# Low parts of weights from VectorE to GpSimd in the second half, and the last quarter's norm factors moved past the first gates

## The chip, the cores and the metric

The kernel runs on one core of a Trainium2 chip. The time is that of one execution on the device in microseconds (us), the median over the runs of a kernel. The engines are TensorE (PE, its weight loads PEld), VectorE (DVE), ScalarE (ACT), GpSimd (POOL) and SyncE (SP), which issues all DMAs. Each engine works through its own queue in order.

## What is computed

One step of a small decoder trunk: a pooling layer (stage A), one projection that gives keys and values to all, and one attention layer (stage B), for 2048 prompt positions and 8 sample positions, model width 1024, 16 heads of 64 in each of three groups of dilation 1, 4 and 16.

```
u, gate = rmsnorm(h, g_a) @ w_a_in                      # 1024 -> 2 x 1024
h = h + (pool_residual(u) @ w_group * scale * silu(gate)) @ w_a_out
kv = rmsnorm(h, g_kv) @ w_kv                            # 1024 -> 3 groups x 2 x 1024, rope on k
q, gate = rmsnorm(h, g_b) @ w_b_in                      # 1024 -> 3 x 1024 + 1024, rope on q
o, lse = windowed attention of each group (128 keys of the block, 128 before)
h = h + (sum over groups of softmax(lse) * o * silu(gate)) @ w_b_out
y = rmsnorm(h, g_final)
```

All is float32. A product runs on TensorE in a shorter float (the type `F32R`) with split operands: each operand is a high part, its rounded copy, and a low part, what the rounding left; a product is high times high, high times low and low times high.

## The kernel before

Activations lie with the width on the partitions, positions along the row. Stage A goes through four quarters of 512 positions (the first with the 8 sample columns). Of each quarter it computes 8 units of `u`, 8 of the gate and, in `run_o`, 8 of the output projection, a unit being one block of 128 output columns: 24 matmuls of 128x512 (eight blocks of the width, three terms). The output of `run_o` is h after the layer; ScalarE squares it, GpSimd adds the squares up in `acc2`, and after the eighth unit `rstd_from` makes of them the factors 1/rms of all positions: four one-column matmuls with a column of ones (L261), a handful of small VectorE instructions around a square root on ScalarE (L262 to L269), a 128x512 diagonal (L270), a matmul that spreads it over the partitions (L280) and a copy (L281). For the last quarter this call was deferred by two ticks, and `close_a` flushes what is deferred, so that it stood between stage A and stage B.

Stage B first takes half 0 (1024 positions): 8 gate units beside which `make_t` builds sums of blocks of the activations (the tiles `t0`, `t1`), then pairs of heads in a form with seven products in place of eight that reads these tiles, then half 1: for each of 8 pairs of heads `p` and three groups units of k, q and v, and 8 gate units at the end. From the last unit of p = 0 on, the attention of the prompt runs beside the units of half 1: at each tick (eight matmuls of a unit, six ticks a unit) one step of `prompt_attn`. A step covers two blocks of 128 queries of one head: score matmuls (L1211, they read the tile `qt`, whose lower half GpSimd copies to the upper partitions in L1163), masking and minimum on VectorE (L1218), exponential on ScalarE (L1224), transposes (L1232), high part on ScalarE (L1244) and low part on VectorE (L1248) of the transposed weights, product with v (L1273 to L1278) and the sum of its two halves on VectorE (L1301).

The weights of a unit come by DMA into a staging tile `wst` of 128x1024, GpSimd scales them by the norm's gain (L127), ScalarE rounds them into `ringh` (L163), and an engine chosen per unit subtracts to get `ringl` (L168). In half 1 there is a single staging tile, so the load of the weights after next waits for L168 of the next. The ring holds the weights of two units. The order within a unit is that of `plan`: at its start the next unit's weights are scaled, one tick later rounded, two ticks later subtracted, and the load of those after next is issued.

```
def lo(self):
    for k in ((0, KT),) if self.eng is pool else ((0, KH2), (KH2, KT)):
        k = slice(*k)
        self.eng.tensor_sub(self.w[1][:, k], self.st[:, k], self.w[0][:, k].bitcast(F32))
...
    at(0, nxt.scale)
    at(int(nxt.gs is not None), nxt.hi)
    at(2 if nxt.gs is not None else 1, nxt.lo)
```

So VectorE does a low part in two instructions of 128x512, GpSimd in one of 128x1024. In stage A the low parts are GpSimd's, in stage B VectorE's. The buffer pool `nwork` has one buffer with the tag `xk`; in stage A `norm_b` uses it, later `make_t` for its temporary `tmp`. The program order written here is not the order on the engines: when the program is built, a list scheduler lays the instructions of each engine out by its own estimate of when they can start, keeping the dependences. A change in one place thus moves instructions in others.

Of the kernel before, what the change touches and what calls it, by code (L numbers as in the profile page):

```python
# [12 lines left out]
F32 = mybir.dt.float32  # L13
# [5 lines left out]
P = 128  # L19
D = 1024  # L20
KT = D // P
SEQ = 2048
NB = 8
HALF = 1024
TOT = SEQ + NB
NQ = 4
QN = SEQ // NQ
# [26 lines left out]
def step_kernel(ctx: ExitStack, tc: tile.TileContext, a: dict):  # L54
    nc = tc.nc
    vec, act, pool, pe = nc.vector, nc.scalar, nc.gpsimd, nc.tensor
# [32 lines left out]
    rpool = low_ctx.enter_context(tc.tile_pool(name="rpool", bufs=1))  # L89
# [3 lines left out]
    rstd2 = {}  # L93
    hn2 = {}
    N = type("N", (), {})()
# [124 lines left out]
    def q_chunks(q):  # L220
        return Q0_CHUNKS if q == 0 else Q_CHUNKS
# [27 lines left out]
    def rstd_from(acc, rstd, n, diag):  # L249
        for _ in rstd_steps(acc, rstd, n, diag):  # L250
            pass
# [36 lines left out]
    def do(fn, *args):  # L288
        items.append(lambda: fn(*args))

    def unit(src, gs, eng, run):
        items.append(Unit(src, gs, eng, run))

    def defer(ticks, fn):
        deferred.append([ticks, fn])
# [18 lines left out]
    def side(gen, rate, name=None):  # L314
        sides.append([gen, rate, 0.0, name])
# [79 lines left out]
    def q_pieces(q):  # L395

        col = q * QN + (NB if q >= 2 else 0)
        return [(col, 0, QN)] + ([(HALF, QN, NB)] if q == 0 else [])

    def q_len(q):  # L400
        return QN + (NB if q == 0 else 0)
# [18 lines left out]
    def work_tile(name, tag="w", bufs=None):  # L420
        return N.work.tile([P, 16 + QN + NB], F32, tag=tag, name=name, bufs=bufs)

    def load_x(q, k):
        xk = work_tile("xk")
        for c0, o, m in q_pieces(q):
            load_dma(xk[:, o:o + m], a["xT"][k, :, c0:c0 + m])
        return xk
# [157 lines left out]
    def run_o(q, ct):  # L585
        def run(w):
            n = q_len(q)
            if ct == 0:
                N.acc2 = work_tile("acc2", "acc", 1)
            xk = load_x(q, ct)  # L590
            acc2 = N.acc2

            def ev(ps, c0, c1):
                vec.tensor_add(xk[:, c0:c1], ps[:, :c1 - c0], xk[:, c0:c1])
                if c1 < n:
                    return
                for d0, o, m in q_pieces(q):
                    store_dma(h1d[ct][:, d0:d0 + m], xk[:, o:o + m])
                if ct == 0:
                    act.activation(acc2[:, :n], xk[:, :n], AF.Square)  # L600
                else:
                    sq = work_tile("sq2")
                    act.activation(sq[:, :n], xk[:, :n], AF.Square)
                    pool.tensor_add(acc2[:, :n], acc2[:, :n], sq[:, :n])
                if ct == KT - 1:
                    r2 = rstd2[q] = rpool.tile([P, QN + NB], F32, tag="rstd2", name="rstd2", bufs=2)
                    defer(2, lambda: rstd_from(acc2, r2, n, work_tile("nv")))
            yield from dense(w, N.y, q_chunks(q), ev, tags=A_TAGS, order=by_term(KT, 0 if ct else 2))
        return run
# [107 lines left out]
    def close_a():  # L717
# [2 lines left out]
        finish()  # L720
        N.actx.close()

    do(close_a)


    def perm(ap, g):
# [102 lines left out]
    def run_qk(hf, kind, g, p):  # L829
        def run(w):  # L830
            raw = raw_tile()
            if kind == 1:
                N.rope = Rope(hf, g)
            rp = N.rope

            def ev(ps, qq, o, m, smpl):
                act.activation(in_order(raw, g, o, m), as_order(ps, g, m), AF.Copy)  # L837
                if smpl:
                    vec.tensor_copy(smp[:, p, kind, g], ps[:, m:m + NB])
                if o + m == HALF:  # L840
                    defer(1, lambda: rp.gather(kind, p, raw))
            yield from dense_h(hf, w, ev)
        return run
# [39 lines left out]
    def run_v(hf, g, p):  # L883
        def run(w):
            vT = [N.bw.tile([P, QN], F32, tag="v", name="vT", bufs=2) for _ in range(2)]

            def ev(ps, qq, o, m, smpl):
                act.activation(vT[qq][:, o - qq * QN:o - qq * QN + m], ps[:, :m], AF.Copy)
                if smpl:
                    vec.tensor_copy(smp[:, p, 2, g], ps[:, m:m + NB])  # L890
                if o + m == (qq + 1) * QN:
                    defer(2, lambda: turn_v(hf, g, p, qq, vT[qq]))
            yield from dense_h(hf, w, ev)
        return run
# [91 lines left out]
    def source(kind, g, p):  # L986
        if kind == 0:
            return a["wQ"][g * NPAIR + p], gq
        return a["wKV"][(2 * g + kind - 1) * NPAIR + p], gvec[:, G_KV]
# [127 lines left out]
    for p in range(NPAIR):  # L1117
        for g in range(3):
            for kind in (1, 0):
                unit(*source(kind, g, p), vec, run_qk(1, kind, g, p))  # L1120
            unit(*source(2, g, p), vec, run_v(1, g, p))
            if p == 0 and g == 2:
                N.attn_unit = sum(not callable(it) for it in items)
                do(start_attention)
# [495 lines left out]
```

## Time and profile before

| | |
|---|---|
| time, median of 3 runs | 3468.94 us (3465.72 to 3475.48) |
| the profiled execution | 3453.65 us, its span 3451.6 us |
| mean granted TensorE clock | 0.969 |
| PE busy | 3187.5 us, 92% of the span |
| DVE, ACT, POOL busy | 2000.7, 1715.3, 1680.1 us (58%, 50%, 49%) |
| mean DMA rate | 173 GB/s |
| half 1 with the attention, 1790 to 3200 us | PE 1338.8 of 1410 us busy, DVE 791.8, ACT 981.2, POOL 712.1 |

A busy share is the share of the time in which an engine has an instruction at work. TensorE's matmuls overlap each other, so that a row's duration is longer than the distance to the next one: eight matmuls of 128x512 in a row take 2.0 us at the full clock.

### The profile page before, as it was taken

What the parts mean: (1) busy time and instruction counts of PE and PEld (TensorE: products, weight loads), DVE (VectorE), ACT (ScalarE), POOL (GpSimd) and SP (SyncE); (2) the same over time, 40 slices, a digit from 0 to 9 for tenths busy, and PEclk for the clock granted to TensorE, in tenths of its full rate; (3) what the DMA queues carried; (4) which work ended last, traced back from release to release, by engine and by line L of the source; (5) the groups of instructions that cost most, each with busy time, mean ns of one, the idle gap of its engine ahead of it and who ended that gap; (6) DMA issues with size and microseconds to landing.
All of it is one profiled execution on the core that took longest, in us unless ns stands there. A gap on an engine that the chain in (4) does not pass through costs nothing.

```text
span 3451.6 us, 56978 instructions
## 1 busy us (share of the span) xinstructions
PE 3187.5 (92%) x19608; PEld 2799.4 (81%) x19608; DVE 2000.7 (58%) x3989; ACT 1715.3 (50%) x3812; POOL 1680.1 (49%) x1026
## 2 busy tenths in 40 slices
PE   8999899899998998987989999999999999999798
PEld 8887678699887887877778877888787888887698
DVE  6745665526767667676426555656464646564345
ACT  3333433324434443334227766776666676778221
POOL 5566765624234354343454454545454645552342
PEclk9999999999999999999999999999999999999899
DMA  4434443434576766767777767687777777774653
GB/s 135 145 129 159 141 156 110 129 98 135 154 185 209 177 193 180 201 198 201 195 206 205 194 187 187 189 201 196 181 194 181 198 182 194 196 199 131 192 155 120
DMA packets 547744, 596.96 MB, mean 173 GB/s; under 512 B 216904, under 2 KB 407752, under 8 KB 547448
## 3 DMA queue, kind: packets, MB, share of 16 engines
q1 hardware_dynamic: 547456, 593.32, 61.7%
q8 instruction: 156, 2.56, 0.3%
q14 instruction: 132, 1.08, 0.1%
HBM read 371.77 MB, written 184.04 MB: 161 GB/s over the span
## 4 chain that ended last, share of the span: by engine, by line
PE 32%; DMA 11%; DVE 5%; ACT 4%; SPq 3%; issue 3%; POOL 2%; DVEq 0%; POOLq 0%; ACTq 0%
PE psd L241 20%; PE pss L1211 3%; PE ppt L1232 3%; PE ppo L1276 1%; PE ppo L1278 1%; DMA spb<-pd 1%; DMA statd<-st 1%; ACT pr L1224 1%; DMA vr<-vd 1%; DMA raw<-xs 1%; DMA qt<-qd 1%; DMA wst<-in_wKV 1%; PE ppo L1273 1%; DVE xs L791 1%; DMA cyt<-yd 1%
## 5 line engine op out<-in xcount | busy, mean ns | idle before, releaser
L1163 POOL CAST qt<-qt 64x1024 fp32r<-64x1024 f32 x192 | 207.1, 1079 | 435.1 <-DMA qt<-qd 371.9
L1224 ACT ACTIVATE pr<-pr,st 128x256 f32<-128x256 f32 (+1 forms) x768 | 345.9, 453 | 126.0 <-DVE st L1218 124.7
L1218 DVE CUSTOM_DVE_ANT_0 pr<-pss,mask 128x256 f32<-128x256 f32 (+1 forms) x768 | 248.5, 360 | 175.7 <-PE pss L1211 118.5
L1248 DVE TENSOR_TENSOR pl<-ppt,ph 128x512 fp32r<-128x512 f32 (+2 forms) x384 | 216.1, 570 | 190.0 <-ACT ph L1244 187.2
L168 POOL TENSOR_TENSOR ringl<-wst,ringh 128x1024 fp32r<-128x1024 f32 x96 | 241.6, 2519 | 124.0 <-ACT ringh L163 72.5
L1211 PE MATMUL pss<-kt,qt 128*128 128x256 f32 (+1 forms) x1536 | 261.2, 288 | 12.8 <-DVE st L1218 7.8
L127 POOL TENSOR_TENSOR wst<-wst,gvec 128x1024 f32<-128x1024 f32 x88 | 177.3, 2017 | 184.8 <-DMA wst<-in_wKV 99.1
L241 PE MATMUL psd<-hn_2h,ringh 128*128 128x512 f32 x640 | 259.2, 405 | 6.6 <-ACT raw L837 5.0
L241 PE MATMUL psd<-hn_3h,ringh 128*128 128x512 f32 x640 | 260.9, 408 | 4.1 <-ACT hn_3h L643 2.4
L163 ACT ACTIVATE ringh<-wst 128x1024 fp32r<-128x1024 f32 x184 | 193.3, 1052 | 139.2 <-PE psd L241 94.9
L241 PE MATMUL psd<-hn_2l,ringh 128*128 128x512 f32 x640 | 257.2, 402 | 5.1 <-DVE hn_2l L644 5.1
L241 PE MATMUL psd<-hn_3l,ringh 128*128 128x512 f32 x640 | 259.4, 405 | 2.5 <-DVE hn_3l L644 2.5
L241 PE MATMUL psd<-hn_2h,ringl 128*128 128x512 f32 x640 | 258.7, 404 | 0.0
L241 PE MATMUL psd<-hn_3h,ringl 128*128 128x512 f32 x640 | 258.4, 404 | 0.0
L1211 PEld LDWEIGHTS pss<-kt,qt 128*128 128x128 f32 x1536 | 223.2, 194 | 29.4 <-DVE st L1218 8.7
L1232 PE MATMUL ppt<-ident,pr 128*128 128x128 f32 x1200 | 209.6, 281 | 36.0 <-DVE pl L1248 23.0
L1244 ACT ACTIVATE ph<-ppt 128x512 fp32r<-128x512 f32 (+2 forms) x384 | 189.7, 500 | 91.6 <-PE ppt L1232 87.1
L168 DVE TENSOR_TENSOR ringl<-wst,ringh 128x512 fp32r<-128x512 f32 x176 | 148.4, 878 | 139.5 <-ACT ringh L163 139.3
L970 PE MATMUL pwx<-t1h,ringh 128*128 128x256 f32 (+1 forms) x576 | 171.1, 297 | 26.4 <-DVE pairl L924 14.0
L1232 PEld LDWEIGHTS ppt<-ident,pr 128*128 128x128 f32 x1200 | 143.1, 142 | 63.1 <-issue 22.5
L1190 POOL TENSOR_TENSOR vt<-vr,vt 128x512 fp32r<-128x512 f32 (+1 forms) x96 | 136.4, 1421 | 80.8 <-ACT vt L1189 72.4
L1276 PE MATMUL ppo<-ph,vt 128*128 128x128 f32 (+1 forms) x688 | 167.6, 274 | 7.6 <-ACT ph L1244 5.7
(301 smaller groups left out, 9828.3 us busy)
## 6 DMA issues: line engine op xcount, KB each, us to landing
qt<-qd SPq DMA_DIRECT2D x192, 256.0 KB
wst<-in_wKV SPq DMA_DIRECT2D x72, 512.0 KB
kt<-kd SPq DMA_DIRECT2D x288, 128.0 KB
wst<-in_wA SPq DMA_DIRECT2D x64, 512.0 KB
wst<-in_wQ SPq DMA_DIRECT2D x52, 512.0 KB
kd<-rh SPq DMA_DIRECT2D x48, 512.0 KB
qd<-rh SPq DMA_DIRECT2D x48, 512.0 KB
vd<-vt SPq DMA_DIRECT2D x96, 256.0 KB
```

Source lines behind the costliest of these rows:

```text
L127: pool.tensor_tensor(st, st, gs[:, :, None].to_broadcast([P, KT, P]), OP.mult)
L163: act.activation(self.w[0], self.st, AF.Copy)
L168: self.eng.tensor_sub(self.w[1][:, k], self.st[:, k], self.w[0][:, k].bitcast(F32))
L241: pe.matmul(ps[:, :n], u[:, k, ws], v[:, k, c0:c1], start=(k, i) == order[0], stop=(k, i) == order[-1])
L1163: pool.tensor_copy(qr[64:128], qr[0:64])
L1211: pe.matmul(ps[:, sl], qt[:, x, qc], kt_[:, kc], start=x == 0, stop=x == 1)
L1218: vec.tensor_tensor_reduce(pr[:, lo:], ps[:, sl], mask[:, lo:], 1.0, BIG, OP.add, OP.min, st[:, 0, h, col:col + 1])
L1224: act.activation(pr[:, lo:], pr[:, lo:], AF.Exp, bias=st[:, 0, h, col:col + 1], scale=-1.0, accum_out=st[:, 1, h, col:col + 1])
L1232: pe.transpose(pt[:, (2 * bb + x) * P:(2 * bb + x + 1) * P], pr[:, x * P:(x + 1) * P], ident)
L1244: act.activation(PB[i][0][:, s], pv[:, s], AF.Copy)
L1248: vec.tensor_sub(PB[i][1][:, s], pv[:, s], PB[i][0][:, s].bitcast(F32))
L1276: pe.matmul(po[:, q0:q1], vt[:, kb + 1, h].rearrange("p x d -> p (x d)"), xh, start=first, stop=False, skip_group_check=True)
```

## The change

In half 1, all units of the pairs of heads with p > 0 (63 units: 7 pairs, three groups, k, q and v) get their low part from GpSimd. The units of p = 0 and the 8 gate units keep VectorE. For the last quarter, the sum of squares and the diagonal get their place in the `xk` buffer of `nwork`, and the norm factors are made by a side generator that starts after `close_a`, lets two ticks pass, issues the sums and the small instructions, waits for three more ticks and issues the spreading matmul and its copy, beside the first gate units.

```diff
             n = q_len(q)
-            if ct == 0:
+            if ct == 0 and q < NQ - 1:
                 N.acc2 = work_tile("acc2", "acc", 1)
+            elif ct == 0:
+                both = N.nwork.tile([P, 2, QN + NB], F32, tag="xk", name="acc3")
+                N.acc2, N.nv3 = both[:, 0], both[:, 1]
             xk = load_x(q, ct)
...
-                if ct == KT - 1:
+                if ct == KT - 1 and q == NQ - 1:
+                    rstd2[q] = rpool.tile([P, QN + NB], F32, tag="rstd2", name="rstd2", bufs=2)
+                elif ct == KT - 1:
                     r2 = rstd2[q] = rpool.tile([P, QN + NB], F32, tag="rstd2", name="rstd2", bufs=2)
                     defer(2, lambda: rstd_from(acc2, r2, n, work_tile("nv")))
...
+    def last_rstd():
+
+        yield
+        yield
+        yield from rstd_steps(N.acc2, rstd2[NQ - 1], QN, N.nv3, 3)
+
     do(close_a)
+    do(lambda: side(last_rstd(), 1.0, "r3"))
...
             for kind in (1, 0):
-                unit(*source(kind, g, p), vec, run_qk(1, kind, g, p))
-            unit(*source(2, g, p), vec, run_v(1, g, p))
+                unit(*source(kind, g, p), pool if p else vec, run_qk(1, kind, g, p))
+            unit(*source(2, g, p), pool if p else vec, run_v(1, g, p))
```

What this does to the engines' queues stands below at three places. Line numbers from L588 on shift by up to 12 in the changed kernel.

TensorE where stage A ends, before: the first gate unit's matmuls (`hn_0`, `hn_1` are the normed activations of the first two quarters), the norm factors, the gate's second half.

```order
L241 MATMUL psd<-hn_0h,ringl 128x264 x8
L261 MATMUL psn<-ones,acc_5203 128x1 x4
L280 MATMUL psn<-nv,ones 128x512
L241 MATMUL psd<-hn_1h_3585,ringh 128x512 x4
L241 MATMUL psd<-hn_1h_3586,ringh 128x512 x4
```

The same place after.

```order
L241 MATMUL psd<-hn_0h,ringl 128x264 x6
L261 MATMUL psn<-ones,acc_5203 128x1 x4
L241 MATMUL psd<-hn_0h,ringl 128x264 x2
L241 MATMUL psd<-hn_1h_3585,ringh 128x512 x4
L241 MATMUL psd<-hn_1h_3586,ringh 128x512 x4
L241 MATMUL psd<-hn_1l_3587,ringh 128x512 x4
L241 MATMUL psd<-hn_1l_3588,ringh 128x512 x4
L241 MATMUL psd<-hn_1h_3585,ringl 128x512 x4
L241 MATMUL psd<-hn_1h_3586,ringl 128x512 x4
L241 MATMUL psd<-hn_0h,ringh 128x256 x8
L241 MATMUL psd<-hn_0l,ringh 128x256 x4
L280 MATMUL psn<-acc_5203,ones 128x512
```

Between the sums (L261) and the spreading matmul (L280) there now stand 24 matmuls of 128x512 and 14 smaller ones; before there was nothing.

VectorE at the same place, before: `make_t` (L668 to L687, its `tmp` in the `xk` buffer) and the norm factors' small instructions. One of the two halves of the `tmp` chain was laid out earlier, in the last quarter of stage A.

```order
L668 TENSOR_TENSOR tmp<-hn_1h_3585,hn_0h 128x2x512
L676 TENSOR_TENSOR tmp<-hn_0h,hn_0l 128x2x8
L669 TENSOR_TENSOR tmp<-tmp,hn_1l_3587 128x2x512
L263 TENSOR_SCALAR rs_5509<-psn 128x4
L670 TENSOR_TENSOR tmp<-tmp,hn_0l 128x2x512
L265 RECIPROCAL rs_5511<-rs_5510 128x4
L266 TENSOR_TENSOR rs_5510<-rs_5511 128x4
L267 TENSOR_TENSOR rs_5510<-rs_5510,rs_5509 128x4
L268 TENSOR_SCALAR rs_5510<-rs_5510 128x4
L269 TENSOR_TENSOR rs_5511<-rs_5511,rs_5510 128x4
L270 TENSOR_TENSOR nv<-ident,rs_5511 128x512
L674 TENSOR_TENSOR tmp<-hn_1h_3586,tmp 128x2x512
```

VectorE after (L673 is what was L668, L690 what was L685).

```order
L270 TENSOR_TENSOR acc_5203<-ident,rs_5590 128x512
L690 TENSOR_TENSOR tmp_5738<-hn_1h_3586,hn_1h_3585 128x1024
L168 TENSOR_TENSOR ringl<-wst,ringh 128x512 x2
L691 TENSOR_TENSOR tmp_5738<-tmp_5738,hn_1l_3588 128x1024
L673 TENSOR_TENSOR tmp<-hn_1h_3585,hn_0h 128x2x512
L681 TENSOR_TENSOR tmp<-hn_0h,hn_0l 128x2x8
L281 COPY rstd_5502<-psn 128x512
L692 TENSOR_TENSOR tmp_5738<-tmp_5738,hn_1l_3587 128x1024
L674 TENSOR_TENSOR tmp<-tmp,hn_1l_3587 128x2x512
L675 TENSOR_TENSOR tmp<-tmp,hn_0l 128x2x512
L168 TENSOR_TENSOR ringl<-wst,ringh 128x512 x2
L679 TENSOR_TENSOR tmp<-hn_1h_3586,tmp 128x2x512
```

The `tmp` chain now begins only behind the norm factors, since these hold the one `xk` buffer until L280 has read it, and both of its halves come after.

GpSimd at the start of the attention, in the second pair of heads, before: scaling (L127), the copies of `qt` (L1163), the low parts of v (L1190) and of rotated k and q (L815).

```order
L127 TENSOR_TENSOR wst<-wst,gvec 128x1024
L1163 COPY qt<-qt 64x1024
L1190 TENSOR_TENSOR vt<-vr,vt 128x10x64
L1163 COPY qt<-qt 64x1024 x2
L127 TENSOR_TENSOR wst<-wst,gvec 128x1024
L1190 TENSOR_TENSOR vt<-vr,vt 128x10x64
L790 TENSOR_TENSOR xs<-xs,cs_5539 128x1024
L1163 COPY qt<-qt 64x1024
L1190 TENSOR_TENSOR vt<-vr,vt 128x8x64
L1163 COPY qt<-qt 64x1024
```

GpSimd after (L1175 is what was L1163, L1202 what was L1190, L827 what was L815).

```order
L127 TENSOR_TENSOR wst<-wst,gq 128x1024
L1202 TENSOR_TENSOR vt<-vr,vt 128x10x64
L1175 COPY qt<-qt 64x1024
L827 TENSOR_TENSOR raw<-raw,rh 128x1024
L1175 COPY qt<-qt 64x1024
L168 TENSOR_TENSOR ringl<-wst,ringh 128x1024
L1175 COPY qt<-qt 64x1024
L1202 TENSOR_TENSOR vt<-vr,vt 128x10x64
L1175 COPY qt<-qt 64x1024 x2
L127 TENSOR_TENSOR wst<-wst,gvec 128x1024
L1202 TENSOR_TENSOR vt<-vr,vt 128x10x64
L1175 COPY qt<-qt 64x1024
```

Per unit there is now one low part (L168) more in GpSimd's queue, with copies of `qt` behind it, and two fewer in VectorE's.

## Rows read from the trace of the kernel before

**Rows 1.** Two stretches: length, busy us (instructions) PE PEld DVE ACT POOL, clock, DMA

```profile
669.00:688.00 19.00, 8.22 (x26) 5.37 (x26) 14.31 (x17) 4.34 (x7) 10.10 (x5) 0.64 0.14 47
1790.00:3200.00 1410.00, 1338.80 (x8400) 1156.40 (x8399) 791.75 (x2383) 981.17 (x2536) 712.12 (x479) 0.98 0.72 188
```

**Rows 2.** Timeline of PE, end of stage A: start, duration, instruction [idle before <-releaser]

```profile
668.19 1.15 PE L241 MATMUL psd<-hn_0h,ringl 128*128 128x264 f32 x8
672.49 1.05 PE L261 MATMUL psn<-ones,acc 128*128 128x1 f32 x8 [3.15 <-POOL acc L604]
679.37 2.07 PE L280 MATMUL psn<-nv,ones 128*128 128x512 f32 x2 [5.82 <-DVE nv L270]
683.24 3.78 PE L241 MATMUL psd<-hn_1h,ringh 128*128 128x512 f32 x8 [1.80 <-ACT sgb L760]
686.82 2.19 PE L241 MATMUL psd<-hn_1l,ringh 128*128 128x512 f32 x8
688.85 2.00 PE L241 MATMUL psd<-hn_1h,ringl 128*128 128x512 f32 x8
```

**Rows 3.** Timeline of POOL, end of stage A

```profile
666.52 2.37 POOL L127 TENSOR_TENSOR wst<-wst,gvec 128x1024 f32<-128x1024 f32 x1 [2.02 <-DMA wst<-in_wQ]
668.85 2.37 POOL L660 TENSOR_TENSOR t1l<-tmp,t1h 128x1040 fp32r<-128x1040 f32 x1
671.19 1.25 POOL L604 TENSOR_TENSOR acc<-acc,sq 128x512 f32<-128x512 f32 x1
```

**Rows 4.** PE's waits, 1790 to 3200 us: total us, times, longest us

```profile
PE ppt L1232 <- DVE pl L1248: 23.0, 15, 4.6
...
PE pss L1211 <- POOL qt L1163: 2.7, 3, 1.5
```

**Rows 5.** Line L660 (ns min/median/max, first to last start), and PE's first read of t0

```profile
L660 POOL TENSOR_TENSOR t1l<-tmp,t1h x4: 2367/2506/3399, 668.9 to 704.7; 128x1040 fp32r<-128x1040 f32 x2, 128x1024 fp32r<-128x1024 f32 x2
...
776.94 0.28 PE L970 MATMUL pwx<-t0h,ringh 128*128 128x256 f32 x1
```

**Rows 6.** DVE by line, 1790 to 3200 us: busy us, mean ns | idle before

```profile
L168 DVE TENSOR_TENSOR ringl<-wst,ringh 128x512 fp32r<-128x512 f32 x136 | 110.4, 848 | 83.0 <-ACT ringh L163 82.9
...
L791 DVE TENSOR_TENSOR xs<-xs 64x1024 f32<-64x1024 f32 x21 | 43.4, 2067 | 25.1 <-POOL xs L790 16.8 <-DMA qt<-qd 6.1 <-DMA kt<-kd 1.7
```

**Rows 7.** Line L168 on GpSimd in stage A, 560 to 669 us

```profile
L168 POOL TENSOR_TENSOR ringl<-wst,ringh x16: 2397/2406/3403, 561.4 to 656.3; 128x1024 fp32r<-128x1024 f32 x16
```

**Rows 8.** Timeline: a low part and its first reader

```profile
2219.89 0.69 DVE L168 TENSOR_TENSOR ringl<-wst,ringh 128x512 fp32r<-128x512 f32 x1 [0.39 <-ACT ringh L163]
...
2243.36 0.40 PE L241 MATMUL psd<-hn_2h,ringl 128*128 128x512 f32 x1
```

**Rows 9.** Timeline: a low part at the attention's start, and its unit

```profile
1796.53 1.29 DVE L168 TENSOR_TENSOR ringl<-wst,ringh 128x512 fp32r<-128x512 f32 x2 [11.98 <-ACT ringh L163]
...
1796.55 0.51 PE L241 MATMUL psd<-hn_2h,ringh 128*128 128x512 f32 x1 [0.81 <-ACT ringh L163]
```

**Rows 10.** Timeline: PE's stalls behind DVE's L168, first, largest and last

```profile
1968.07 0.44 PE L1232 MATMUL ppt<-ident,pr 128*128 128x128 f32 x2 [0.48 <-DVE pl L1248]
...
2558.83 0.45 PE L1232 MATMUL ppt<-ident,pr 128*128 128x128 f32 x1 [2.46 <-DVE pl L1248]
...
3010.99 0.41 PE L1232 MATMUL ppt<-ident,pr 128*128 128x128 f32 x2 [0.42 <-DVE pl L1248]
```

**Rows 11.** The stretch around it (columns as in Rows 1)

```profile
2552.00:2566.00 14.00, 9.65 (x45) 8.10 (x46) 10.57 (x30) 10.76 (x30) 10.66 (x7) 0.63 0.73 208
```

**Rows 12.** Timeline: a copy of qt and its first reader

```profile
2221.03 1.05 POOL L1163 CAST qt<-qt 64x1024 fp32r<-64x1024 f32 x1 [1.00 <-DMA qt<-qd]
...
2228.98 0.50 PE L1211 MATMUL pss<-kt,qt 128*128 128x128 f32 x3
```

**Rows 13.** Timeline of POOL and DVE before the largest of them

```profile
2553.50 2.36 POOL L815 TENSOR_TENSOR raw<-raw,rh 128x1024 fp32r<-128x1024 f32 x1 [0.59 <-DMA o_k<-raw]
...
2554.72 3.36 DVE L168 TENSOR_TENSOR ringl<-wst,ringh 128x512 fp32r<-128x512 f32 x2 [1.63 <-ACT ringh L163]
```

## The prediction

> **What bounds the kernel now.** The page's shares come first: TensorE is busy 92% of the span, so time can only be won where it stands still or runs at the lower of its two clock levels (1.2 instead of 2.4 GHz). The view by stretches then tells how much of that each stage holds. In half 1 with the attention beside it, 1790 to 3200 us, PE is busy 1338.8 of 1410 us: 71 us idle, and a granted clock of 0.98 is another 28 us. The 19 us where stage A ends are the densest loss of the kernel: 8.2 us busy, clock 0.64 [rows 1]. The change touches these two places and no other.
>
> At the end of stage A the timeline shows who ends each wait. PE finishes its last product at 668.19 + 1.15 = 669.34 and begins the next at 683.24: 13.9 us. In between it waits 3.15 us for GpSimd's last sum of squares, 5.82 us for VectorE's diagonal and 1.80 us for ScalarE, whose evacuation of a bank stood behind the square root [rows 2]. The last sum came late because GpSimd had a scaling and a low part of `make_t` ahead of it [rows 3]. In half 1 the waits of PE are many and short; the largest total is on VectorE's low part of the attention weights, 23.0 us in 15 times, while waits on GpSimd's copies of `qt` are 2.7 us in 3 times [rows 4].
>
> **Part 1: the norm factors.** Nothing is computed less; four one-column sums, one square root with its table loads, six small VectorE instructions, a diagonal, a spreading matmul and a copy move from between two products to beside them. No DMA moves. Goes: 13.9 us of standstill, and the lower clock behind it, where eight matmuls take 3.78 and 2.19 us instead of 2.00 [rows 2]: 1.78 + 0.19 = 2.0 us. Together 15.9 us. Stays: the sums and the spreading matmul themselves, about 1.0 us at the full clock (an estimate: the rows' 1.05 and 2.07 us are each two records of one piece of work at the lower clock). Added: PE now meets the sums two matmuls before the first gate's first half ends, at about 669.1. GpSimd's low part of `make_t` no longer stands before the last sum of squares, which would so end at 666.52 + 2.37 + 1.25 = 670.1 [rows 3]: a wait of 1.0 us, with the rest of the gate behind it. The spreading matmul stands 24 products of 128x512 and 14 smaller ones later, some 7 us (eight of 128x512 take 2.00 us, eight of 128x264 1.15 [rows 2]); the chain from sums to diagonal took 679.37 - 672.49 - 1.05 = 5.8 us with instructions of `make_t` in between [rows 2], so that wait goes. Sum: -15.9 + 1.0 + 1.0 = -13.9 us.
>
> What pays for it is `make_t`: its temporary shares the buffer that the factors now hold until about 678 us, so its whole chain comes later. Behind its first instruction VectorE queues the gates' own low parts. One half of the chain plus the two short ones took from 668.9 + 2.4 to 704.7 + 2.4 us, 36 us [rows 5]; even two such lengths from 678 end at 750. The first product that reads `t0` starts at 776.94 [rows 5], about 763 after the gain. I cost it at nothing; without that cover each us of lateness is a us of PE.
>
> **Part 2: the low parts in half 1.** 63 units. VectorE loses 126 instructions of 848 ns mean [rows 6], 107 us; GpSimd gains 63 of 2.41 us [rows 7], 152 us, and goes from 712 to 864 of 1410 us. Neither engine is the bound, so these sums are not the gain. Off the path: a low part of a running unit ends 2243.36 - 2219.89 - 1.3 = 22 us before its first reader [rows 8], 16 us as the median over the 80 units. 1.1 us more (2.41 against two of 0.69 less their overlap) and a few copies ahead in the queue are covered. Not covered: the three or four units at the start of the attention, where the low part ends with the unit already running, because ScalarE rounded so late [rows 9]; GpSimd's single instruction must also be whole before the first low product, where VectorE's two let PE start on the first half. 4 units at 0 to 2 us; I take 2 us.
>
> What goes on PE: of its stalls in this stretch, seven end on VectorE with a low part (L168) in VectorE's queue in the 6 us before. They sum to 6.8 us, from 0.48 at 1968.07 to 0.42 at 3010.99, the largest 2.46 us at 2558.83 [rows 10]. Around that one the clock falls to 0.63 over 14 us, 5.2 us lost [rows 11]. VectorE also stands 82.9 us before low parts, waiting for ScalarE's rounding [rows 6], with the attention's masks and low parts behind; I count no more for it than the stalls show, since PE covers such waits with products. The bounds of the gain: 0, and half of all that is lost in the stretch, (71 + 28)/2 = 50 us, if the attention's chain as a whole tightens. I take 6.8 + 5.2 = 12 us, what these rows show.
>
> What comes on GpSimd: behind each low part stand copies of `qt`, behind these the scores on PE. A copy ends 6.9 us before its first reader as the median of the 192 (one of them: 2222.08 to 2228.98 [rows 12]); 14 of the 192 have less than 2.4 us. If every one of the 192 came 2.4 us later, PE would stand 17.6 us more in sum; for one in three (63 of 192), 5.8 us. If all came 3.7 us later, because GpSimd also waits for ScalarE's rounding as VectorE did (82.9/63 = 1.3 us each), it would be 42 us. Bounds 0 and 42; I take 4, under the 5.8 since GpSimd mostly stands idle before a copy, waiting for its DMA. The load of the weights after next, which SP issues when the low part is done, moves by the same 1.1 us, with q and k loads behind it in SP's queue; the same 6.9 us cover it. Sum of part 2: -12 + 2 + 4 = -6 us.
>
> A low part on VectorE takes 848 ns in the mean and 0.69 us alone [rows 6, 8]; the 0.16 us between them have a cause in the trace. VectorE's low part at 2554.72 took 3.36 us for two instructions of 0.69, and its first half ended only after GpSimd's subtraction of 2553.50 to 2555.86 [rows 13]. The Trainium skill, page "SBUF — State Buffer", section "Who interferes with whom", says that a VectorE instruction with both inputs in SBUF and a GpSimd instruction that reads SBUF exclude each other for a whole instruction; this row agrees. By that rule the moved low parts would in turn hold up VectorE's other instructions of that kind; it is the fourth rival below.
>
> **The sum.** -13.9 - 6 = -20 us on the profiled execution of 3453.65 us (span 3451.6 and 2 around it), 3434. That execution lies 15 us under the median of the three timed runs, so I carry the difference: 3469 - 20 = 3449 us.
>
> **The rivals.** (1) Only the boundary pays: GpSimd's delays eat VectorE's relief, part 2 is 0: 3469 - 14 = 3455. For it: PE waits for VectorE's low parts of the attention mostly without an L168 near. (2) GpSimd becomes the late engine: copies of `qt` wait behind low parts that wait for ScalarE. It turns the total to slower from 0.4 us of PE standstill per moved low part on (14 + 10.4 = 24 us over 63); at 42 us the time is 3469 - 14 + 42 = 3497, at the middle of its range, 30 us, 3485. For it: GpSimd's queue is in order and 46 of 192 copies have under 5 us; against it: only 2.7 us of such waits now, and GpSimd idle half the time. (3) The attention's chain tightens: VectorE no longer stands 82.9 us before low parts, half of the stretch's loss goes: 3469 - 14 - 40 = 3415. (4) The blocking changes sides: L791, 21 instructions of 2067 ns [rows 6], each held 2.41 us longer, 51 us on VectorE; PE paid a third of such time so far (6.8 of 126 x 0.16 = 20 us), 17 us: 3449 + 17 = 3466. (5) The boundary does not do what it says, since `make_t` or the gates' low parts behind it come late and PE stands as long a little further on: 3469 - 6 = 3463.
>
> **How the numbers follow.** Forecast 0.45, own range 3439 to 3458; rival 1 0.24; 2 0.12; 3 0.09; 4 0.04; 5 0.06. The range 3420 to 3472 leaves out most of rival 2 and about half of 3, some 0.17. What a measurement tells from no change here is 0.3%, 10.4 us, so faster means under 3458.5 and slower above 3479.3. Faster: 0.43 of the forecast, 0.15 of rival 1, all of 3, a little of 5: 0.69. Slower: 0.10 of rival 2 and 0.01 of others: 0.11. The rest, 0.20, is within.
>
> **What would show it.** Right: no pause over 2 us between the first gate's two halves, the clock there at 1.00, L261 waiting about 1 us and L280 not at all; the first read of `t0` without a wait on `make_t`; in half 1 fewer than 71 us of PE idle, PE's wait on VectorE's L1248 under 23 us and its wait on `qt` under 9 us; POOL near 860 us there. Wrong: a wait of PE on `ringl` from GpSimd, or on `qt` of 20 us and more; PE waiting for `t0l`; half 1 ending later relative to its start than 1410 us. The forecast fails if half 1 moves by more than 20 us either way, for then an effect that the stalls of now do not show decides.

## The result and the profile after

The changed kernel is slower: 3616.07 us (3613.71 to 3617.25) against 3472.21 us for the kernel before on the same chip, ratio 1.043 [1.042, 1.045], 144 us. The prediction said 3449 us, in a range that ended at 3472, and gave slower a chance of 0.11. It was wrong, in its sign too.

The profiled execution places the loss. First the stretch where stage A ends and the whole stage with the attention, from the first scores to the last dense unit, by the view of stretches (columns as in [rows 1]); in the kernel before, this stage is the second fence.

```profile
669.00:688.00 19.00, 16.49 (x96) 14.60 (x95) 13.40 (x18) 6.60 (x10) 7.14 (x4) 0.91 0.33 114
1803.00:3371.00 1568.00, 1415.00 (x8410) 1198.73 (x8411) 689.13 (x2266) 971.24 (x2525) 840.57 (x538) 0.95 0.66 168
```

```profile
1805.00:3209.00 1404.00, 1333.61 (x8380) 1152.74 (x8379) 791.15 (x2383) 979.22 (x2533) 707.83 (x476) 0.98 0.71 187
```

The attention stage is 164 us longer, and so is the whole profiled execution; the medians are 144 us apart, since the profiled execution of the kernel before lies under its median. PE does the same matmuls; its idle time goes from 70 to 153 us, and its busy time grows by another 81, at a clock of 0.95 instead of 0.98. VectorE is relieved of 102 us and GpSimd has 133 us more, as intended; both are busy for only about half of the stage. The 19 us at the end of stage A are better, 16.5 us busy instead of 8.2 [rows 1].

The waits of PE in the stage (total us, times, longest us), to be held against [rows 4]; L1260 is what was L1248, L1236 the exponential, L1256 the high part, L1201 the high part of v:

```profile
PE ppt L1244 <- ACT pr L1236: 31.7, 27, 6.7
PE ppo L1288 <- ACT ph L1256: 20.4, 15, 5.2
PE ppt L1244 <- DVE pl L1260: 20.4, 35, 2.1
PE ppo L1288 <- DVE ot L1313: 13.3, 11, 4.3
PE psd L241 <- ACT ringh L163: 12.3, 9, 2.9
...
PE ppo L1285 <- ACT vt L1201: 7.2, 2, 5.0
...
PE psd L241 <- POOL ringl L168: 1.7, 1, 1.7
...
PE pss L1223 <- POOL qt L1175: 1.1, 2, 0.7
```

The kernel before has, from 1805 to 3209 us,

```profile
...
PE ppt L1232 <- ACT pr L1224: 8.7, 10, 3.7
...
PE ppo L1276 <- ACT ph L1244: 5.7, 6, 2.1
...
PE ppo L1276 <- DVE ot L1301: 1.8, 1, 1.8
```

PE waits 2.8 us for the engine that got the work. What has grown are waits in the attention's own chain, transposes for exponentials (8.7 to 31.7 us), products for high parts and for output sums, and those for ScalarE's rounded weights (`ringh`). The wait on the attention's low parts, the largest of before, has not grown (23.0 to 20.4). A timeline of PE shows how such a stretch looks (start, duration, instruction, [idle before <-releaser]):

```profile
2642.68 0.39 PE L241 MATMUL psd<-hn_3l,ringh 128*128 128x512 f32 x1
2642.91 1.10 PE L1223 MATMUL pss<-kt,qt 128*128 128x128 f32 x8
...
2644.96 0.52 PE L1244 MATMUL ppt<-ident,pr 128*128 128x128 f32 x3 [0.52 <-DVE pl L1260]
...
2647.38 0.52 PE L1244 MATMUL ppt<-ident,pr 128*128 128x128 f32 x3 [0.38 <-DVE pl L1260]
...
2648.84 0.33 PE L1288 MATMUL ppo<-ph,vt 128*128 128x128 f32 x1 [0.71 <-ACT ph L1256]
2649.04 1.17 PE L1223 MATMUL pss<-kt,qt 128*128 128x128 f32 x8
2650.06 0.60 PE L1244 MATMUL ppt<-ident,pr 128*128 128x128 f32 x4
...
2651.46 0.33 PE L1244 MATMUL ppt<-ident,pr 128*128 128x128 f32 x1 [0.34 <-ACT pr L1236]
2651.95 0.44 PE L1244 MATMUL ppt<-ident,pr 128*128 128x128 f32 x2 [0.16 <-ACT pr L1236]
2653.25 0.41 PE L1244 MATMUL ppt<-ident,pr 128*128 128x128 f32 x2 [0.86 <-DVE pl L1260]
2654.03 0.44 PE L1244 MATMUL ppt<-ident,pr 128*128 128x128 f32 x2 [0.38 <-ACT pr L1236]
2654.23 0.48 PE L241 MATMUL psd<-hn_2h,ringl 128*128 128x512 f32 x1
```

From 2642.91 to 2654.23 there is no dense matmul (L241) at all, only pieces of the attention and four transposes of a unit of v. Seven of the rows shown wait for something to come back from VectorE or ScalarE, 3.35 us together. In the built programs this can be counted. The columns are the kernels; e2 to e14 are the experiments below.

| TensorE's built order | before | after | e2 | e8 | e13 | e14 |
|---|---|---|---|---|---|---|
| no dense matmul between the scores of two steps, of 383 places | 119 | 171 | 175 | 107 | 184 | 201 |
| more than 24 of them there | 2 | 37 | 38 | 1 | 37 | 29 |
| transposes under 2 us of TensorE work behind their scores (an estimate, by columns at 2.4 GHz), of 384 steps | 8 | 83 | 87 | 8 | 108 | 22 |

The dense matmuls stand in long runs and the attention's pieces in bunches between them. SyncE's order moved too: of the 96 loads of v, 10 before and 35 after stand behind three or more loads of q that belong to their own or a later chunk.

### The profile page after: what moved, and what is told of

Its sections match the earlier page's. It is cut to its first block, busy times and chain, and to the rows that moved or that the text cites. A ratio compares the mean times of both kernels' runs of the same rounds, so it can differ in the third digit from the quotient of the medians.

```text
span 3615.5 us, 56753 instructions
## 1 busy us (share of the span) xinstructions
PE 3268.1 (90%) x19608; PEld 2846.5 (79%) x19608; DVE 1898.6 (53%) x3863; ACT 1707.9 (47%) x3804; POOL 1811.4 (50%) x1089
## 4 chain that ended last, share of the span: by engine, by line
PE 46%; DMA 18%; DVE 12%; SPq 7%; ACT 7%; issue 6%; POOL 4%; DVEq 0%; ACTq 0%; POOLq 0%
PE psd L241 29%; PE pwx L982 4%; DMA vr<-vd 3%; PE pss L1223 3%; PE ppt L1244 2%; PE pwy L982 2%; ACT pr L1236 2%; DMA spb<-pd 2%; DMA xk<-in_xT 2%; DVE xs L803 2%; PE pwv L982 1%; DVE sw L535 1%; SPq L795 1%; SPq L796 1%; SPq L794 1%
## 5 line engine op out<-in xcount | busy, mean ns | idle before, releaser
L168 POOL TENSOR_TENSOR ringl<-wst,ringh 128x1024 fp32r<-128x1024 f32 x159 | 392.0, 2467 | 188.5 <-ACT ringh L163 124.9
L1260 DVE TENSOR_TENSOR pl<-ppt,ph 128x512 fp32r<-128x512 f32 (+2 forms) x384 | 217.6, 572 | 356.5 <-ACT ph L1256 350.5
L1236 ACT ACTIVATE pr<-pr,st 128x256 f32<-128x256 f32 (+1 forms) x768 | 345.6, 452 | 97.6 <-DVE st L1230 96.8
L1175 POOL CAST qt<-qt 64x1024 fp32r<-64x1024 f32 x192 | 205.6, 1074 | 306.5 <-DMA qt<-qd 234.6
L241 PE MATMUL psd<-hn_2h,ringh 128*128 128x512 f32 x640 | 270.4, 422 | 20.0 <-ACT ringh L163 12.3
L127 POOL TENSOR_TENSOR wst<-wst,gvec 128x1024 f32<-128x1024 f32 x88 | 177.3, 2018 | 214.4 <-DMA wst<-in_wKV 151.9
L1244 PE MATMUL ppt<-ident,pr 128*128 128x128 f32 x1200 | 228.0, 291 | 59.9 <-ACT pr L1236 31.7
L241 PE MATMUL psd<-hn_2h,ringl 128*128 128x512 f32 x640 | 273.1, 427 | 3.3 <-POOL ringl L168 2.9
L241 PE MATMUL psd<-hn_2l,ringh 128*128 128x512 f32 x640 | 266.4, 416 | 5.1 <-DVE hn_2l L649 5.1
L241 PE MATMUL psd<-hn_3h,ringh 128*128 128x512 f32 x640 | 259.9, 406 | 10.1 <-ACT vT L900 4.6
L241 PE MATMUL psd<-hn_3l,ringh 128*128 128x512 f32 x640 | 258.5, 404 | 2.2 <-DVE hn_3l L649 2.2
L241 PE MATMUL psd<-hn_3h,ringl 128*128 128x512 f32 x640 | 257.4, 402 | 0.0
L1223 PE MATMUL pss<-kt,qt 128*128 128x256 f32 (+1 forms) x1536 | 249.2, 296 | 4.3 <-DVE st L1230 2.8
L1256 ACT ACTIVATE ph<-ppt 128x512 fp32r<-128x512 f32 (+2 forms) x384 | 188.9, 499 | 103.2 <-PE ppt L1244 94.3
L1288 PE MATMUL ppo<-ph,vt 128*128 128x128 f32 (+1 forms) x688 | 167.7, 281 | 33.9 <-ACT ph L1256 20.4
L1202 POOL TENSOR_TENSOR vt<-vr,vt 128x512 fp32r<-128x512 f32 (+1 forms) x96 | 131.3, 1368 | 132.2 <-ACT vt L1201 112.6
L982 PE MATMUL pwx<-t1l,ringh 128*128 128x256 f32 (+1 forms) x576 | 169.0, 293 | 0.0
```

The lines of the kernel that those rows point to most:

```text
L127: pool.tensor_tensor(st, st, gs[:, :, None].to_broadcast([P, KT, P]), OP.mult)
L241: pe.matmul(ps[:, :n], u[:, k, ws], v[:, k, c0:c1], start=(k, i) == order[0], stop=(k, i) == order[-1])
L982: pe.matmul(ps[:, :c1 - c0], u[:, k], v[:, k, c0:c1], start=(first and k == 0 and j == 0), stop=(k == KH2 - 1 and j == 2), skip_group_chec ...
L1175: pool.tensor_copy(qr[64:128], qr[0:64])
L1223: pe.matmul(ps[:, sl], qt[:, x, qc], kt_[:, kc], start=x == 0, stop=x == 1)
L1236: act.activation(pr[:, lo:], pr[:, lo:], AF.Exp, bias=st[:, 0, h, col:col + 1], scale=-1.0, accum_out=st[:, 1, h, col:col + 1])
```

## The experiments

The tool of most of them is a second build. The program is built once, the order of chosen engines is noted, and it is built again with each noted instruction tied behind its predecessor on the same engine. This holds the issue order and adds no wait between engines:

```
for x, y in zip(order[e], order[e][1:]):
    tc.add_manual_dep(traced[e][y], traced[e][x].name, mybir.DependencyInfo(
        mybir.DependencyClass.NoSync, mybir.DependencyReason.DATA), reason="order")
```

The ties alone were not measured on the kernel before; e6 and e8 below, one tied and one free, both without the moved low parts, lie 1 us apart.

"The low parts" are those of pairs 1 to 7 of half 1, as in the change; where orders are held, they alone are not tied. An engine whose order is not held is laid out anew by the scheduler. Differences in us are between medians of one series.

| run | low parts | order held | against before | us |
|---|---|---|---|---|
| e1 norm factors alone | VectorE | | 0.9966 [0.9948, 0.9984] | -12.5 |
| e2 low parts alone | GpSimd | | 1.0421 [1.0397, 1.0444] | +146 |
| e3 | GpSimd | PE of before | 1.0239 [1.0209, 1.0268] | +83 |
| e4 | VectorE | PE of e2 | 1.0436 [1.0412, 1.0460] | +152 |
| e5 | GpSimd | all of before | 1.0057 [1.0036, 1.0077] | +20 |
| e6 | left out | all of before | 0.9971 [0.9955, 0.9986] | -10 |
| e7 change whole | GpSimd | all of e1 | 1.0028 [1.0013, 1.0043] | +9 |
| e8 | left out | | 0.9968 [0.9952, 0.9983] | -11 |
| e9 | GpSimd | PE, DVE of before | 1.0240 [1.0206, 1.0273] | +79 |
| e10 with norm factors | halves | all of e1 | 0.9976 [0.9962, 0.9990] | -9 |
| e11 | GpSimd | PE, ACT of before | 1.0244 [1.0221, 1.0267] | +84 |
| e12 | GpSimd | PE, SP of before | 1.0103 [1.0077, 1.0129] | +33 |
| e13 | GpSimd | SP of before | 1.0281 [1.0255, 1.0307] | +95 |
| e14 | VectorE | all of before, PE bunched by hand | 1.0153 [1.0118, 1.0187] | +49 |

**e1 and e2: the two parts apart.**

```diff
-                unit(*source(kind, g, p), pool if p else vec, run_qk(1, kind, g, p))
+                unit(*source(kind, g, p), vec, run_qk(1, kind, g, p))
```

(e1, from the changed kernel, and the same for v; e2 is the kernel before with only these two lines as changed.)

> The last quarter's norm factors are beside the first gates, all low parts of half 1 stay on VectorE. In the built programs TensorE's order in half 1 is row for row that of before. All theories that blame the low parts: the 7 to 10 us that the trace of after shows at the boundary (gates of half 0: 99.4 us before, 89.9 after; start of the pairs 7.3 us earlier) stay, so 3462 us (3458 to 3466) against 3472. Theory 'the norm factors upset what follows': 3560 or more, with the attention stage near 1568 us as in after.

> Only the low parts of pairs 1 to 7 of half 1 go to GpSimd; the norm factors stay where they were. Theories that blame the low parts: the loss of after (144 us) and the 9 us of the boundary that it no longer has, 3472 + 144 + 9 = 3625 us (3605 to 3640). Theory 'the norm factors upset what follows': 3475 or less.

Measured -12.5 and +146 us. The norm factors do what they were meant to, and the low parts bring the loss.

**e3 and e4: work and order exchanged.** e3 has e2's work in TensorE's order of before, e4 the work of before in TensorE's order of e2.

> The low parts on GpSimd as in e2, but every TensorE instruction stands in the order of before (only issue order is held, no wait is added; the other engines' orders are free). Theory ORDER (the loss comes from transposes that now stand closer behind their scores on TensorE: median 4.1 us of TensorE work between them at full clock, 6.1 before; under 2 us in 87 of 384 steps against 8): the loss goes, 3440 to 3490 us, and half 1's stalls fall back to those of before. Theory GPSIMD (the extra 340 us of work on GpSimd, its late low parts or the contention that it brings cost it whatever the order): 3580 us or more, as in e2.

> All low parts on VectorE as in before, but every TensorE instruction stands in the order of e2. Theory ORDER: the loss is there without any work moved, 3590 to 3650 us. Theory GPSIMD: 3465 to 3490 us, as before.

e4 is the clearest run of the study: no work has moved, and the loss is there, +152 us. GpSimd's work is thus not needed for it. The other engines' orders, SyncE's too, were free to follow it. e3 hit neither theory: 3542 us lies between the 3490 of the one and the 3580 of the other. TensorE's order was not all. (The 340 us of work in my expectation for e3 are wrong: GpSimd is busy 1680.1 us before and 1815.8 in e5, 136 more.)

**e5 and e6: all five orders held.** e6 issues no low part in these pairs.

```diff
-            for k in ((0, KT),) if self.eng is pool else ((0, KH2), (KH2, KT)):
+            for k in () if self.eng is None else ((0, KT),) if self.eng is pool else ((0, KH2), (KH2, KT)):
```

> Low parts of pairs 1 to 7 on GpSimd as in e2, and now not TensorE alone but VectorE, ScalarE, GpSimd and SyncE issue everything else in the order of before; only the low parts themselves are free to stand where the scheduler puts them in GpSimd's queue. Theory ORDER (e3's remaining 83 us are the orders of the other engines, which were free there): 3440 to 3475 us, and by the prediction's own terms for this part (6 us of gain in the layout of before) 3453. Theory GPSIMD (the moved work itself, late or in the way, is worth e3's 83 us): 3520 to 3550, with TensorE waits for ringl or vt or qt from GpSimd that sum to tens of us.

> The low parts of pairs 1 to 7 of half 1 are left out (their matmuls read what stands in the ring), everything else stands in the order of before on all engines. VectorE is relieved of 126 instructions and GpSimd gets none. Theory ORDER: 3440 to 3460 us, about e5. Theory GPSIMD: also 3440 to 3460, so that e5 minus this run is what GpSimd's work costs: under 15 us by ORDER, 70 us or more by GPSIMD.

+20 and -10 us: e5 is a shade over ORDER's range (3477 for 3475) and far under GPSIMD's, but e5 less e6 is 30 us, twice what ORDER allowed. In the old order the moved work is worth 20 us of loss in place of 146. Its trace shows part of it, in the timeline of PE, all where the attention begins:

```profile
1797.48 0.80 PE L241 MATMUL psd<-hn_2h,ringl 128*128 128x512 f32 x1 [1.00 <-POOL ringl L168]
1814.98 0.50 PE L241 MATMUL psd<-hn_2h,ringl 128*128 128x512 f32 x1 [4.06 <-POOL ringl L168]
1835.73 0.50 PE L241 MATMUL psd<-hn_2h,ringl 128*128 128x512 f32 x1 [1.13 <-POOL ringl L168]
1858.90 0.50 PE L241 MATMUL psd<-hn_2h,ringl 128*128 128x512 f32 x1 [3.30 <-POOL ringl L168]
```

These four are 9.5 us. Of its waits from 1790 to 3350 us:

```profile
...
PE ppt L1232 <- DVE pl L1248: 15.7, 11, 5.3
PE psd L241 <- POOL ringl L168: 9.5, 4, 4.1
...
PE pss L1211 <- POOL qt L1163: 2.3, 1, 2.3
```

The profiled executions of e5 and e6 are only 17.5 us apart, the medians 30.

**e7 and e8: the whole change in the old order, and what makes the scheduler lay it out anew.** e8 leaves the low parts out and holds nothing.

> The changed kernel whole (norm factors and low parts), with the orders of e1 held on all five engines and only the low parts free in GpSimd's queue. Theory ORDER: the sum of e1 (-12 us) and e5 (+20), so before + 8: 3465 us (3450 to 3480), that is 150 us less than the changed kernel with its own orders. Rival (the two parts together do something that neither does alone): 3500 us or more.

> The low parts of pairs 1 to 7 of half 1 are left out as in e6, and the scheduler is free on all engines. It tells what in the edit makes the order worse. Rival RELIEF (VectorE without these 126 instructions lets the scheduler put the transposes closer to their scores): 3550 us or more. Rival PLACE (it is their place in GpSimd's queue that makes the scheduler bunch the dense matmuls; in the built order more than 24 dense matmuls lie between the scores of two steps in 1 of 383 places here, 2 before, 38 in e2): 3430 to 3465 us, like e6.

e7: +9 us, where the sum of e1 and e5 was +8; the same instructions on the same engines as in the changed kernel, about 135 us sooner. e8: -11 us, its order as evenly mixed as before (table above). So it is not VectorE's relief but the low parts' place on GpSimd that makes the scheduler bunch. In built orders the bunching grows with it: transposes under 2 us behind their scores are 13, 22, 50, 75 and 87 where the last 1, 2, 4, 6 and 7 pairs are GpSimd's. That the scheduler counts on the low parts later there than on VectorE, and lays attention ahead of the dense matmuls meanwhile, would explain this; it is argued, not shown.

**e9, e11 and e12: whose order is it besides TensorE's?**

> As e3 (low parts on GpSimd, TensorE's order held), and VectorE's order held too; ScalarE, GpSimd and SyncE are free. It tells whose order makes e3 65 us slower than e5. If VectorE's (in e3 TensorE waits 33.1 us for the output sums ot of VectorE, 12 times): 3465 to 3500 us. If ScalarE's, GpSimd's or SyncE's: 3520 to 3550 us.

> As e3 (low parts on GpSimd, TensorE's order held), and ScalarE's order held too; VectorE, GpSimd and SyncE are free. If ScalarE's order makes the 65 us that e3 has over e5 (in e9 ScalarE waits 102.9 us, 41 times, for the rows of v that its splits read, 68.0 and 28 times before, with exponentials and high parts queued behind): 3465 to 3495 us. If not: 3515 to 3545 us.

> As e3, and SyncE's order held too; VectorE, ScalarE and GpSimd are free. If SyncE's order makes the 65 us (loads of q, k and v queue behind issues that wait for scores or transposes: 105.0 and 76.1 us in e9, 79.4 and 50.9 before): 3465 to 3495 us. If neither this run nor e11 falls under 3500, it is GpSimd's order or several together.

My guesses for VectorE (+79) and ScalarE (+84) failed; both runs stand where e3 stands. SyncE's order takes 50 of the 83 us away. GpSimd's order was not held by itself; with ScalarE's and VectorE's it makes up the 13 us that e12 lies above e5, little beside intervals of 18 and 14 us. PE's waits on `qt`, 2.3 us in e5, are part of these; in e12 they are (1812 to 3241 us)

```profile
PE pss L1211 <- POOL qt L1163: 19.1, 7, 7.0
```

One thing that SyncE's order does is seen at the rows of v, which ScalarE splits. ScalarE's waits for them (1790 to 3350 us) in the kernel before, in e3 and in e12:

```profile
ACT vt L1189 <- DMA vr<-vd: 68.0, 28, 9.0
```

```profile
ACT vt L1189 <- DMA vr<-vd: 98.8, 31, 7.4
```

```profile
ACT vt L1189 <- DMA vr<-vd: 62.1, 25, 6.8
```

But late rows of v are not what the 50 us consist of. In e11 and in e4, whose SyncE order was free too and which lose 84 and 152 us, the same waits are

```profile
ACT vt L1189 <- DMA vr<-vd: 72.6, 23, 8.4
```

```profile
ACT vt L1189 <- DMA vr<-vd: 69.9, 28, 9.6
```

close to those of before; by the count above 17 loads of v are late in e11, 8 in e4, 25 in e3. Which transfers make the 50 us stays open. In the changed kernel these waits are 151.7 us in 57 times. One of them in its timeline of SP, of ACT and of PE: the load of v is issued behind two loads of k (L1171) and six for the rotation (L794 to L796), before the first of which SyncE had stood 4.9 us for ScalarE, and PE stands 5 us for it.

```profile
2304.18 0.56 SPq L794 DMA_DIRECT2D xs<-raw  x1
...
2308.20 0.50 SPq L1171 DMA_DIRECT2D kt<-kd  x1
2308.80 0.53 SPq L828 DMA_DIRECT2D qd<-raw  x1
2309.37 0.49 SPq L1171 DMA_DIRECT2D kt<-kd  x1
2309.96 0.80 SPq L1195 DMA_DIRECT2D vr<-vd  x1
...
2316.17 0.63 ACT L1201 ACTIVATE vt<-vr 128x512 fp32r<-128x512 f32 x1 [4.11 <-DMA vr<-vd]
...
2316.85 0.37 PE L1285 MATMUL ppo<-ph,vt 128*64 128x128 f32 x1 [5.03 <-ACT vt L1201]
```

**e13 and e14: bunching or the order of the transfers?** e13 leaves TensorE's order free and holds SyncE's. e14 moves no work: it takes the orders of before and rearranges TensorE's alone (`first` has the places of each step's first score matmul, `psd` is the tile of the dense matmuls).

```
for a, b in list(zip(first, first[1:]))[::2]:
    order[a:b] = sorted(order[a:b], key=lambda k: name(k) != "psd")
```

> Low parts on GpSimd, SyncE's order (all DMA issues) held as before, the other four engines free. TensorE's built order is as bunched as in e2 or more: transposes under 2 us behind their scores in 108 of 384 steps (87 in e2, 8 before), no dense matmul between the scores of two steps in 184 of 383 places (175 in e2, 119 before). Theory BUNCH (bunched work on TensorE costs by itself): 3570 us or more, like e2. Theory SYNC (the order of the DMA issues costs, TensorE's order only brings it along): 3510 us or less.

> All low parts on VectorE, the orders of before on all engines, and TensorE's changed in one way: from every second step's scores to the next step's, the dense matmuls go first and the attention's pieces after them (no dense matmul between the scores of two steps in 201 of 383 places, more than 24 in 29; transposes under 2 us behind their scores in 22 of 384). Theory BUNCH: 60 us or more slower than before, 3520 us or more. Theory SYNC: 3480 us or less.

Both fell between the two theories: +95 and +49 us. So there are two causes. With the low parts on GpSimd, the four combinations are:

| | SyncE's order of before | SyncE's order free |
|---|---|---|
| TensorE's order of before | +33 (e12) | +83 (e3) |
| TensorE's order free (bunched) | +95 (e13) | +146 (e2) |

Bunching costs 62 or 63 us, the order of transfers 50 or 51, whichever way one goes. The near equality is partly luck: each of the four intervals is 16 to 20 us wide, and a free order is not the same in two runs (e13's TensorE order has 108 close transposes, e2's 87). Nor does the split hold beyond this table: e4, with e2's TensorE order and no work on GpSimd, loses 152 us, not some 60. SyncE's order was free there, and e2's TensorE order with SyncE's order of before was not run, so what each of them costs in e4 is open. The stage's rows of e12, e3, e13 and e14 tell the two apart:

```profile
1812.00:3241.00 1429.00, 1339.39 (x8396) 1159.71 (x8394) 705.28 (x2268) 976.32 (x2532) 831.85 (x535) 0.98 0.69 183
```

```profile
1816.00:3294.00 1478.00, 1356.60 (x8378) 1168.69 (x8377) 700.32 (x2265) 974.84 (x2530) 833.22 (x532) 0.96 0.66 176
```

```profile
1800.00:3310.00 1510.00, 1393.86 (x8417) 1181.06 (x8416) 685.69 (x2261) 984.55 (x2538) 836.40 (x536) 0.96 0.66 174
```

```profile
1805.00:3255.00 1450.00, 1351.63 (x8380) 1163.71 (x8379) 793.72 (x2382) 975.99 (x2533) 709.57 (x477) 0.97 0.68 181
```

Late transfers (e3 against e12) are mostly standstill: idle 90 to 121 us, busy +17. Bunching (e13 against e12) is mostly slower work: idle 90 to 116, busy +54 (these two profiled executions are 80 us apart, the medians 62). e14 against before is idle 70 to 98 and busy +18, with no work on GpSimd and with few close transposes (22 under 2 us): bunching needs neither to cost.

**e10: a version in search of the gain.** VectorE does the first four blocks of a low part and GpSimd, beside it, the last four.

```diff
+                eng = pool if self.eng == "both" and k[0] else vec if self.eng == "both" else self.eng
                 k = slice(*k)
-                self.eng.tensor_sub(self.w[1][:, k], self.st[:, k], self.w[0][:, k].bitcast(F32))
+                LOWS.add(eng.tensor_sub(self.w[1][:, k], self.st[:, k], self.w[0][:, k].bitcast(F32)).ins.name)
```

> A version in search of the gain: norm factors beside the gates as in e1, the orders of e1 held on all engines, and of each low part in pairs 1 to 7 VectorE makes the first four blocks as before and GpSimd the last four, which TensorE reads twelve matmuls later. If e5's 30 us over e6 are low parts that come too late, half of them made in parallel are not late, and half of the relief of e6 stays: before - 12 - 5 = 3440 us (3430 to 3448), under e1. If they are GpSimd getting in VectorE's way or delaying its other work, 3455 to 3465.

(`LOWS` lists the low parts, which are not tied.) -9 us [-13, -3]: 3444.53 us lies in the first reading's range of 3430 to 3448, but against the kernel before, some 4 us faster in this series, it is not the -17 us of that reading, and no better than e1. The second reading's 3455 or more did not come. Against whole low parts on GpSimd (e7, +9) halves win 18 us. Being late can be a good part of the 30 us, but halves also leave GpSimd half of the work, so this is argued and not shown; the hoped-for 5 us did not come. e1, the norm factors alone, is the simplest version that beats both kernels: 3446.14 us (3434.72 to 3458.57).

## Why the prediction was wrong

**The step that failed** is the second part, "Sum of part 2: -12 + 2 + 4 = -6 us". All three of its terms were read from waits in the order of before, and all three are costs of moved work in that order. What decided is that the order does not stay: the text on the kernel says that a list scheduler lays out every engine anew, I showed its new rows for TensorE and VectorE where stage A ends and for GpSimd in half 1, and did not look at TensorE's or SyncE's in half 1, where the counts of the first table could have been had beforehand. The runs put there, in place of -6: +20 for the work in the old order (e5), +13 for the free orders of ScalarE, VectorE and GpSimd (e12 less e5), +50 for SyncE's, +63 for TensorE's, together e2's +146 (they add up because each is the difference to the run before; taken in another order the shares may differ). My list of what would make the forecast fail had the right sentence, that half 1 moving by more than 20 us means an effect that the stalls of now do not show, but no rival carried it and no chance was set on it.

Term by term, in the order in which they were meant to hold (e5, e6): the stalls of PE behind VectorE's low parts were to lose 6.8 us, and the total of [rows 4] falls from 23.0 to 15.7 us in e5 and 10.2 in e6. With the clock 12 us; all that the relief is worth is 10 [5 to 16] (e6). That term was right in its size. The first units at the attention's start: I took 2 us out of 0 to 8, and the trace of e5 has four waits of 9.5 us together, at the place I named, more than the 8 that I had as the most. Copies of `qt`: I took 4 out of 0 to 42, and PE's waits there are 2.3 us, 2.7 before. The term was too large. So the sum for the old order, -6 us, was off by 26 even there; the 9.5 us account for a part, and the rest of e5's 30 us over e6 is in no wait of PE that I can name and stays open.

**The boundary** was right in its mechanism and nearly in its size. The timeline of PE in the changed kernel, against [rows 2]:

```profile
671.80 1.05 PE L261 MATMUL psn<-ones,acc 128*128 128x1 f32 x8 [0.52 <-POOL acc L607]
672.72 0.49 PE L241 MATMUL psd<-hn_0h,ringl 128*128 128x264 f32 x2
673.04 2.00 PE L241 MATMUL psd<-hn_1h,ringh 128*128 128x512 f32 x8
...
682.12 1.12 PE L280 MATMUL psn<-acc,ones 128*128 128x512 f32 x2 [1.99 <-DVE acc L270]
...
769.63 0.28 PE L982 MATMUL pwx<-t0h,ringh 128*128 128x256 f32 x1
```

The sums wait 0.52 us, for which I had 1.0. The spreading matmul still waits 1.99 us for the diagonal, where I had written off that wait, and the clock over the 19 us is 0.91 and not 1.00. The first read of `t0` waits for nothing, as said. I forecast -13.9 us; e1 measures -12.5. In the changed kernel nothing of it is left to be seen in the total (after 1.043, e2 1.042), although it is in the trace of this place. By the profiled executions the lead is gone where the attention begins, at 1803 us against 1802 in e2, and the stage with the attention, in another bunched order, takes 1568 us against e2's 1554.

**The rivals.** "Only the boundary pays" and "The boundary does not do what it says" kept the old order too. "GpSimd becomes the late engine" had the right sign and the wrong mechanism: PE's waits on `qt` are 1.1 us in the changed kernel and 19.1 at most, in e12. "The attention's chain tightens" is what TensorE's new order does, with the sign turned: packed closer together, the chain is exposed. "The blocking changes sides" asked for L791 to be held 2.41 us longer each time. The trace of e5 has, to be held against [rows 6],

```profile
L791 DVE TENSOR_TENSOR xs<-xs 64x1024 f32<-64x1024 f32 x21 | 44.7, 2126 | 41.5 <-POOL xs L790 19.2 <-DMA kt<-kd 16.4 <-DMA qt<-qd 5.7
```

That is 59 ns more on each, 1 us in all, and against e6 (1947 ns) 4 us; in the changed kernel the mean is 1559 ns. The cost of that rival did not come. The blocking was weighed from the Trainium skill, page "SBUF — State Buffer", section "Who interferes with whom"; that VectorE and GpSimd exclude each other is not tested further here, and in the old order e5 less e6 bounds all that the moved work can do at 30 us.

Two theories of my own fell on the way: that transposes close behind their scores are all of it (e14 has few of them and still loses 49 us, e12 to e3 adds none and loses 50), and that VectorE's or ScalarE's order makes the rest of e3 (e9, e11).

## What to carry to other kernels

Where a scheduler lays out the program, the first question to an edit is not what the work costs but what else it moves: compare the built order of the engine that bounds the kernel, and of the DMA issues, before any wait is costed, and count how evenly its independent work is mixed with the chain that has to wait for other engines. If the two orders differ, hold the old one by ties of issue order and measure the edit in it; here that turned a loss of 146 us into one of 20, and showed that there were only some 10 us to win. That an engine has time to spare, as GpSimd had, says nothing on this.

## What the runs showed of the hardware beside this

Bunched work costs TensorE twice. From e12 to e13 its idle time rises by 26 us and its busy time, for the same matmuls, by 54; the granted clock over the stage goes from 0.98 to 0.96. But it is 0.96 in e3 too, with TensorE's order of before, and there the busy time is only 17 us above e12's: the clock is a part of the 54 at most. The rest I cannot split further: that small matmuls in a bunch overlap less with each other than with dense ones is one reading, not tested. In e14 it is the other way round, 28 us more of idle time and 18 of busy time than before.
